# Shifting the SBUF start addresses of the dense products' operands in a hybrid RWKV-7 / Conformer backbone

## The chip, the cores and the metric

The kernel runs on one core of a Trainium2 chip. The metric is the device time of one execution in microseconds (us). The kernel before was run three times: 1453.27, 1447.48 and 1452.06 us, median 1452.06. One more execution was taken with the hardware profiler; it is the one that all traces of the kernel before show.

Engines are named as the profile names them: PE is TensorE's matrix product, PEld its weight load, DVE is VectorE, ACT is ScalarE, POOL is GpSimd, SP is SyncE.

## The reference

Two layers over 512 latent tokens of width 1024, with 256 context tokens. Layer 0 (even) is a bidirectional RWKV-7 scan beside a gated short convolution; layer 1 (odd) is a Conformer convolution module. Cut to what matters here:

```python
# layer 0
r, k, v, za, bg, cg, xb, zb = jnp.split(h @ w_in, EVEN_SPLITS, axis=-1)     # 1024 -> 8 * 1024
ya, _, _ = rwkv_seq(rwkv_prep(h, r, k, v, *rw), S_f, S_b, r_k, lnx_w, lnx_b, True)
yb = bg * dwconv(cg * xb, sc_w, seg_len)
y = jnp.concatenate([ya * jax.nn.silu(za), yb * jax.nn.silu(zb)], axis=-1) @ w_out   # 2048 -> 1024
...
# layer 1
u, gl, z = jnp.split(h @ w_in, 3, axis=-1)                                  # 1024 -> 3 * 2048
a = u * jax.nn.sigmoid(gl)
a = dwconv(a, dw_w, seg_len) + dw_b                                         # 31 taps, segments of 64
a = layer_norm(a, ln_w, ln_b)
return (jax.nn.silu(a) * jax.nn.silu(z)) @ w_out                            # 2048 -> 1024
```

Each layer is wrapped in RMS norms with shift, scale and gate, and the context tokens take part in layer 0 as the scan's prefix.

## The kernel before

**Split-value products.** Most dense products are made from operands that are split into a high part, rounded to the type fp32r, and a low part, the rest (`hilo`, L121). `mm3` (L59) makes one product from three matmuls: high x high, high x low, low x high, all into one PSUM bank. `mm(o, lhsT, rhs)` (L56) issues one matmul: `lhsT` is the stationary operand, which a weight load brings into the array, and `rhs` is the moving operand, which is streamed past it. The trace writes a matmul as output <- moving, stationary. A dense product moves 512 columns past a 128x128 weight (256 columns for the context). While one matmul streams, the next one's weights are loaded.

**Stages, in the order of the program.**
- Start: norms, modulation, and the low-rank projections of layer 0.
- Layer 0's projections (`proj`, L361). The weights are loaded, split (`load_w`, L356) and stationary; the split input `hlat` (`hlh`, `hll`, L201) moves. Outputs are named `plr`, `plk`, `plv`, `pza`, `pcg`, `pxb`, `pbg`, `pzb`, and `pck`, `pcv` for the context. From about 200 us they are placed between the small matmuls of the scan (`chain_ctx`, `chain_lat`, L738), which run chunk by chunk for eight pairs of heads.
- Layer 0's output projection in two halves (`outproj`, L130, output `o`): the weights `wh`, `wl` move, the activations `y` are stationary.
- Layer 1's input projection of `u` and `gl` (`products`, L1119, output `pu`): four column blocks n times four token blocks m, 48 matmuls each; the weights `wc..` move, `h1h` and `h1l` are stationary.
- The 31-tap convolution as a transform, a product and a transform back (`dft_stages`, L1085), one (n, m) block behind the products: `forward` (output `px`) with stationary `dfc` (its high part `dfh` and its low part `dfl`) and moving `ah`, then `back` (output `pc`). `late` takes one of the two after each half of `products`.
- Transposes (`at`), then layer 1's `z` projection in 16 column blocks (L1186, output `pz`): the weights `wz..` are stationary and `h1h`, `h1l` move. Block 0's weights come from the pool tag `wb`, those of blocks 1 to 15 from the tag `wz`.
- The last projection (L1215, output `f`): the weights `wf..` move, the 16 activations `y` are stationary; the first ten of these lie in the tag `wb`, the others in `xr`.

**Forward transform.** `ah` holds 64 tokens of one segment as a high part in one half of its 128 rows and as a low part in the other half; `dfc` holds the same 64 rows of the transform twice. For each of two segments s, one matmul of `dfh` over all 128 rows gives high x (high + low), and one of `dfl` over 64 rows gives low x high. The two 64-row matmuls use different halves of the rows.

**What sets the order.** Within a stage the order of PE is that of the code; some products are held to a written order (`pinned`) or to an anchor (`issue_after`). A weight load or a matmul waits by semaphore for the casts of its operands.

**What sets the addresses.** A tile's start in SBUF, in bytes within each partition, follows from the pools: each pool takes tiles one after another, the pools `cp`, `cvp`, `wk` and `lp` from the left end, `hlp`, `wp`, `op` and `lq` from the right end. One float more or less in a tile shifts all that come after it. These are the places of the dense products' operands in the program before, as the start of the operand modulo 128 bytes:

| output | matmuls | moving | stationary |
|---|---|---|---|
| projections of the latent tokens | 1536, 512 columns | 96 | 96 |
| projections of the context | 384, 256 columns | 96 | 96 |
| `lwl`, `lal` (low-rank weights) | 64 | 96 | 64 |
| `o` | 372 (and 12 others) | 96 | 96 (64 and 32) |
| `pu` | 768 | 32 | 64 |
| `px` high | 32 | 64 | 64 |
| `px` low | 32, of 64 rows | 64 | 28 |
| `pz` block 0 | 24 | 64 | 32 |
| `pz` blocks 1 to 15 | 360 | 64 | 64 |
| `f`, first ten activations | 240 | 64 | 32 |
| `f`, last six | 144 | 64 | 96 |

The small fp32 matmuls of the scan read most operands at 64 or 0, and some, the tiles `E` among them, at 32 or 96.

Of the kernel before, what the change touches and what calls it, by code (L numbers as in the profile page):

```python
# [8 lines left out]
F32 = mybir.dt.float32  # L9
F32R = mybir.dt.float32r  # L10
# [5 lines left out]
P = 128  # L16
# [12 lines left out]
NPROD = 119  # L29
# [22 lines left out]
def kernel(ctx: ExitStack, tc: tile.TileContext, I: dict, out: bass.AP):  # L52
    nc = tc.nc
    V, S, G, T = nc.vector, nc.scalar, nc.gpsimd, nc.tensor
# [4 lines left out]
    def mm3(o, ah, al, bh, bl, start, stop, go=mm):  # L59
        go(o, ah, bh, start, False)  # L60
        go(o, ah, bl, False, False)
        go(o, al, bh, False, stop)
# [4 lines left out]
    def const(name, shape, dt=F32):  # L67
        return cp.tile(shape, dt, tag=name, name=name)

    ident = const("ident", [P, P])  # L70
    epsr = const("epsr", [P, 3])
    G.memset(epsr[:, 0:1], RMS_EPS)
    G.memset(epsr[:, 1:2], LN_EPS)
    G.memset(epsr[:, 2:3], GN_EPS)
    nc.sync.dma_start(ident, I["ident"])

    colsrc = {
# [40 lines left out]
    def bank(name, tag):  # L118
        return ps.tile([P, 512], F32, tag=tag, name=name, bufs=2 if tag in ("at", "zo") else 1)

    def hilo(src, raw, hi, lo, eng=nc.sync):  # L121
        if eng:
            eng.dma_start(raw if len(src.shape) == 2 else raw.rearrange("p (k c) -> p k c", c=src.shape[2]), src)
        else:
            raw = src
        S.copy(hi, raw)  # L126
        env["lo"].tensor_tensor(out=lo, in0=raw, in1=hi, op=ALU.subtract)  # L127
        return hi, lo

    def outproj(m0, tags, ks, held, early=lambda k: (None, None, None), between={}):  # L130
        acc = [[bank(f"o{m0 + m}{n}", tags[2 * m + n]) for n in range(2)] for m in range(2)]
        for k in ks:
            y, yr, ws = early(k)
            if y is None:
                y = op.tile([P, 512], F32R, tag="y", name=f"y{m0}_{k}", bufs=4)
            yh, yl = y[:, 0:256], y[:, 256:512]
            if (m0, k) == (0, 7):
                hilo(oT7[:, 0:256], None, yh, yl, None)
            else:
                if yr is None:  # L140
                    yr = op.tile([P, 256], F32, tag="yr", name=f"yr{m0}_{k}", bufs=4)
                hilo(ysp[k, :, m0 * P : m0 * P + 2 * P], yr, yh, yl)
            if k not in held:
                if ws is None:
                    ws = [op.tile([P, D], F32, tag="wr", name=f"wr{m0}_{k}", bufs=3)] + [
                        op.tile([P, D], F32R, tag="w", name=f"w{x}{m0}_{k}", bufs=6) for x in "hl"]
                held[k] = hilo(wo[k * P : (k + 1) * P, :], *ws)
            wh, wl = held[k]
            for m in range(2):
                ms = slice(m * P, (m + 1) * P)  # L150
                for n in range(2):
                    ns = slice(n * 512, n * 512 + 512)
                    mm3(acc[m][n], yh[:, ms], yl[:, ms], wh[:, ns], wl[:, ns], k == ks[0], k == ks[-1])
            if k in between:
                between[k]()
        return acc
# [10 lines left out]
    def ps_at(name):  # L167
# [3 lines left out]
    hlp = rs.enter_context(tc.tile_pool(name="hlp", bufs=1, reuse_waits="tile", side="right"))  # L171
# [2 lines left out]
    NBUF = {"tmp": 3, "bon": 3, "AR": 6, "BK": 2, "BKt": 4, "UV": 2, "E": 2, "PC0": 4, "PC1": 4, "rnq": 2,  # L174
            "H": 2}
    SIZE = {"AR": D, "BK": 1536, "BKt": D, "UV": 2 * D, "O": 768, "X": D, "E": 4 * D, "P": 528, "H": 256, "HP": 256,
            "h0": 256, "PC0": 8, "PC1": 8, "rnq": 48, "xtmp": 136}

    def w(tag, name, dt=F32):
        return wk.tile([P, SIZE.get(tag, 512)], dt, tag=tag, name=name, bufs=NBUF.get(tag, 1))  # L180
# [4 lines left out]
    def small(name, shape):  # L185
        return cvp.tile(shape, F32, tag=name, name=name)

    ones = small("ones", [P, 1])
    G.memset(ones, 1.0)
    omu, hmu, hka, oka = (small(n, [P, k]) for n, k in (("omu", 24), ("hmu", 24), ("hka", 8), ("oka", 8)))  # L190
    owa, hwa = (small(n, [P, 16]) for n in ("owa", "hwa"))
    blk = small("blk", [P, P])
# [6 lines left out]
    ss6 = small("ss6", [P, 16])  # L199
    lorl = [[cvp.tile([P, SEQ], F32R, tag=f"{t}{z}", name=f"{t}{z}") for z in range(2)] for t in ("tanhl", "xal")]  # L200
    hlat = tuple(hlp.tile([P, KT, SEQ], F32R, tag=t, name=t) for t in ("hlh", "hll"))  # L201
    E0 = w("E", "hctx", F32R).rearrange("p (a k c) -> p a k c", a=2, k=KT)
    hch, hcl = E0[:, 0], E0[:, 1]
    E1 = w("E", "ectx")
# [356 lines left out]
    def pinned():  # L561
        prev = []

        def go(o, lhsT, rhs, start=True, stop=True, op=mm):
            e = op(o, lhsT, rhs, start, stop)
            if prev:
                tc.add_manual_dep(e.ins, prev[-1].name,
                                  mybir.DependencyInfo(mybir.DependencyClass.NoSync, mybir.DependencyReason.DATA),
                                  reason="written order")
            prev[:] = [e.ins]  # L570
            return e

        return go
# [344 lines left out]
    for s in range(12):  # L918
# [10 lines left out]
        for x in STAGE[s >= 4]:  # L929
# [17 lines left out]
            elif x == "C":  # L947
                conv_branch(s - 3, st["anchor"])
                if s == 10:
                    rs.close()  # L950
                    op = rs.enter_context(tc.tile_pool(name="op", bufs=1, reuse_waits="tile", side="right"))
# [20 lines left out]
    def early(k):  # L972
        i = ORDER.index(k)
        tag = etags[i] if i < len(etags) else None
        if tag is None:
            return None, None, None
        y = yr = None
        if i < 4:
            y = w(("kk", "kd", "a", "P")[i], f"ye{k}", F32R)[:, 0:512]
            yr = w(("lwl", "k_", "r_", "lwl")[i], f"yre{k}")[:, 0:256]  # L980
        if tag == "E":
            if not eE:
                e = w("E", "wE", F32R)
                eE.extend([e[:, (2 * j + x) * D : (2 * j + x + 1) * D] for x in range(2)] for j in range(2))
            hl = eE.pop(0)
        else:
            hl = [w(tag, f"we{k}{x}", F32R) for x in "hl"]
        return y, yr, [w("BK", f"wre{k}")[:, 0:D]] + hl

    acc0 = outproj(0, ("mm0", "mm1", "at", "at"), ORDER, held, early)  # L990
    l0.close()
    with ExitStack() as l1:
        lp = l1.enter_context(tc.tile_pool(name="lp", bufs=1, reuse_waits="tile"))
# [2 lines left out]
        def lt(tag, name, dt=F32):  # L996
            return (lq if tag in ("xr", "pr") else lp).tile([P, 512 if tag in ("a", "pr") else D], dt, tag=tag, name=name,
                                                            bufs=BUFS[tag])
# [5 lines left out]
        def big(name, shape, dt=F32):  # L1004
            return lp.tile(shape, dt, tag=name, name=name)
# [10 lines left out]
        def gate_rows(layer):  # L1016
            g = lq.tile([P, D], F32, tag="gg", name="gg1") if layer else lt("wz", "gg0")
            nc.gpsimd.dma_start(g, gvd[layer].unsqueeze(0).to_broadcast([P, D]))
            return g
# [42 lines left out]
        gg = gate_rows(0)  # L1062
        ordered = []
        dfw = lt("a", "dfw")[:, :NPROD]
        dfc = big("dfc", [P, 2 * NPROD + 2], F32R)
        dfh, dfl = dfc[:, :NPROD], dfc[:, NPROD : 2 * NPROD]
        dbe = big("dbe", [P, 8])[:NPROD, 0:1]
        dinv = big("dinv", [NPROD, 64])
        nc.gpsimd.dma_start(dfw, I["dfw"])
        S.copy(dfh, dfw)  # L1070
# [10 lines left out]
        tp = pinned()  # L1081
# [3 lines left out]
        def dft_stages(n, m, ahl):  # L1085
            pr = [lt("pr", f"pr{n}{m}{s}") for s in range(2)]

            def forward():
                px = [bank(f"px{n}{m}{s}", "zo") for s in range(2)]
                for s in range(2):  # L1090
                    tp(px[s][:NPROD], dfh, ahl[s], True, False)
                for s in range(2):
                    tp(px[s][:NPROD], dfl[64 * s : 64 * s + 64, :], ahl[s][64 * s : 64 * s + 64, :], False, True)
                for s in range(2):
                    V.scalar_tensor_tensor(out=pr[s][:NPROD], in0=px[s][:NPROD], scalar=dbe[:, 0:1],  # L1095
                                           in1=What[:, n * 512 : n * 512 + 512], op0=ALU.add, op1=ALU.mult)

            def back():
                pc = bank(f"pc{n}{m}", "at")
                for b in range(2):  # L1100
                    bs = slice(256 * b, 256 * b + 256)
                    for s in range(2):
                        tp(pc[64 * s : 64 * s + 64, bs], dinv, pr[s][:NPROD, bs])
                cr = cres[m][n // 2][:, (n % 2) * 512 : (n % 2) * 512 + 512]
                S.copy(cr, pc)
                V.bn_stats(stats[:, m, n, :], cr)

            return forward, back
# [44 lines left out]
        lq = rs.enter_context(tc.tile_pool(name="lq", bufs=1, reuse_waits="tile", side="right"))  # L1153
# [47 lines left out]
            ys.append((yh, yl))  # L1201
        w2 = I["od_w_out"][0]
        gg = gate_rows(1)
        xres = [lt("wa", f"xo{m}") for m in range(4)]
        for m in range(4):
            nc.gpsimd.dma_start(xres[m], x1d[m])
# [119 lines left out]
```

## Time and profile before

| | |
|---|---|
| three runs, median | 1452.06 us (1447.48 to 1453.27) |
| profiled execution, its own time | 1451.59 us |
| profiled execution, span from first to last instruction | 1449.6 us |
| mean granted TensorE clock | 0.979 |

The span is the time between the first and the last instruction; the execution's own time is 2.0 us longer. Stages by the first start of their matmuls: `pck` at 48.7 us, `pcg` from 489.6 us, `o` from 929.0 us, `pu` from 1040.2 us, `pz` from 1255.5 us, `f` from 1353.4 us. The last store ends the span at 1449.6 us.

Durations of single matmuls in the trace overlap, since the next one starts before the last column of the one before has left the array, and their ends are modelled. How fast a stream of matmuls runs is therefore read from start to start, or from the length of a run of them on the chain divided by their count.

### The profile page before, as it was taken

The page shows a single profiled execution, that of the slowest core. Times are in us where ns is not written, and L with a number is a line of the kernel's source. Part 1 is how long each engine was busy: PE and PEld are TensorE (multiplying, and loading weights), DVE is VectorE, ACT ScalarE, POOL GpSimd, SP SyncE. Part 2 cuts the span into 40 slices and gives each one's busy share as a digit, 9 for nine tenths or more (in the row PEclk, how much of TensorE's full clock was granted, in tenths as well). Part 3 has the DMA queues.
Part 4 walks back from the last instruction along what each step waited for, and adds up shares of the span by engine and source line. Part 5 has one row for each costly group of instructions (what it writes and reads, how often), then busy time and mean ns, then how long its engine had stood idle before and what let it go on. Part 6 is the DMA issues. An engine that isn't in the chain of part 4 may idle for free. (4 is left out here: it accounts for less than half of the span.)

```text
span 1449.6 us, 29729 instructions
## 1 busy us (share of the span) xinstructions
PE 1407.2 (97%) x11921; PEld 1012.7 (70%) x11921; DVE 983.7 (68%) x2294; ACT 749.5 (52%) x1516; POOL 118.2 (8%) x246
## 2 busy tenths in 40 slices
PE   6999999999998999999999999999999999999998
PEld 1564677878776766666676666778777777788876
DVE  2675597568688989999999998557745544544333
ACT  4536364364664665756666565456753323464222
POOL 2023210000101101011011100010000000000000
PEclk9999999979897999999999999999999999999999
DMA  9755433312222321222222212359803303133322
GB/s 324 221 172 160 153 110 98 97 52 71 83 85 74 92 69 59 81 86 60 76 67 83 91 49 84 131 175 324 252 34 102 117 22 95 58 102 91 99 89 86
DMA packets 137626, 158.54 MB, mean 109 GB/s; under 512 B 15375, under 2 KB 104143, under 8 KB 137369
## 3 DMA queue, kind: packets, MB, share of 16 engines
q1 hardware_dynamic: 121104, 106.47, 23.6%
q0 software_dynamic: 15312, 48.99, 10.5%
q8 instruction: 94, 1.54, 0.4%
q10 hardware_dynamic: 1072, 1.19, 0.2%
q14 instruction: 44, 0.36, 0.1%
HBM read 138.33 MB, written 18.28 MB: 108 GB/s over the span
## 5 line engine op out<-in xcount | busy, mean ns | idle before, releaser
L57 PE MATMUL o<-wh,y 128*128 128x512 f32 x248 | 79.7, 397 | 0.0
L658 DVE TENSOR_TENSOR Yl<-Yl,xtmpl 128x126 f32<-128x126 f32 (+22 forms) x248 | 62.2, 251 | 2.7
L656 DVE TENSOR_TENSOR xtmpl<-Xl,Yl 128x126 f32<-128x126 f32 (+22 forms) x248 | 62.0, 250 | 2.7
L57 PE MATMUL pal<-ARl,BKl 64*128 64x128 f32 x512 | 57.8, 306 | 5.5 <-DVE xtmpc L656 2.8
L57 PEld LDWEIGHTS pal<-ARl,BKl 64*128 64x128 f32 x512 | 42.9, 195 | 24.9 <-issue 6.0
L1140 ACT CAST ah<-a 64x512 fp32r<-64x512 f32 x32 | 19.8, 619 | 75.6 <-DVE a L1135 75.2
L57 PE MATMUL zol<-UV,E 64*64 64x64 f32 (+1 forms) x1024 | 54.0, 221 | 0.2 <-ACT UV L764 0.2
L57 PEld LDWEIGHTS o<-wh,y 128*128 128x128 f32 x248 | 45.9, 188 | 9.5
L764 ACT COPY UV<-uh 64x128 f32<-64x128 f32 x128 | 33.3, 260 | 33.5 <-PE uh L57 25.9
L57 PE MATMUL o<-wl,y 128*128 128x512 f32 x124 | 49.4, 398 | 1.2 <-DVE wl L127 1.2
L57 PE MATMUL zol<-Hl,ARl 64*64 64x64 f32 x896 | 50.2, 230 | 0.3
L57 PEld LDWEIGHTS zol<-Hl,ARl 64*64 64x64 f32 x896 | 35.0, 133 | 20.3 <-issue 16.7
L127 DVE TENSOR_TENSOR wl<-wr,wh 128x1024 fp32r<-128x1024 f32 x28 | 34.2, 1223 | 19.6 <-ACT wh L126 19.1
L1135 DVE TENSOR_TENSOR a<-pu,a 128x512 f32<-128x512 f32 x16 | 11.0, 690 | 53.0 <-PE pu L57 50.7
L57 PEld LDWEIGHTS uh<-UV,BKt 128*64 128x64 f32 x704 | 26.7, 138 | 28.5 <-ACT UV L764 23.1
L601 DVE TENSOR_TENSOR E<-pal,maskE 128x512 f32<-128x512 f32 x64 | 43.0, 685 | 3.4 <-PE pal L57 3.0
L57 PEld LDWEIGHTS zol<-UV,E 64*64 64x64 f32 (+1 forms) x1024 | 42.3, 136 | 2.5 <-ACT UV L764 2.0
L1095 DVE SCALAR_TENSOR_TENSOR pr<-px,dbe,What 119x512 f32<-119x512 f32 x32 | 22.6, 745 | 31.1 <-PE px L57 31.1
L126 ACT CAST wh<-wr 128x1024 fp32r<-128x1024 f32 x28 | 29.6, 1056 | 20.7 <-PE o L57 10.4
L771 DVE SCALAR_TENSOR_TENSOR Hl<-uh,PCl,HPl 128x64 f32<-128x64 f32 x112 | 26.4, 277 | 20.1 <-PE uh L57 9.6
L875 POOL DMA_DIRECT2D mwr<-in_mod_w_dram x56 | 29.9, 538 | 114.2 <-PE uh L57 67.4
L57 PE MATMUL uh<-UV,BKt 128*64 128x64 f32 x704 | 36.7, 234 | 2.2 <-ACT UV L764 2.2
(947 smaller groups left out, 4250.9 us busy)
## 6 DMA issues: line engine op xcount, KB each, us to landing
mwr<-in_mod_w_dram POOLq DMA_DIRECT2D x56, 256.0 KB, 3.6
wr<-in_ev_w_out_dram SPq DMA_DIRECT2D x28, 512.0 KB, 5.6
ectx<-in_mod_w_dram SPq DMA_DIRECT2D x12, 512.0 KB, 5.2
wrk<-in_ev_w_in_dram SPq DMA_DIRECT2D x16, 256.0 KB, 3.1
wrv<-in_ev_w_in_dram SPq DMA_DIRECT2D x16, 256.0 KB, 4.6
wrr<-in_ev_w_in_dram SPq DMA_DIRECT2D x16, 256.0 KB, 2.9
wrza<-in_ev_w_in_dram SPq DMA_DIRECT2D x16, 256.0 KB, 2.8
wrcg<-in_ev_w_in_dram SPq DMA_DIRECT2D x16, 256.0 KB, 2.8
```

What stands on the lines that cost most here:

```text
L57: return T.matmul(o, lhsT, rhs, start=start, stop=stop)
L126: S.copy(hi, raw)
L127: env["lo"].tensor_tensor(out=lo, in0=raw, in1=hi, op=ALU.subtract)
L601: V.tensor_tensor(out=E[:, h, z * NLAT + c0 : z * NLAT + c0 + m, :], in0=pas[h], in1=maskE[:, z * (1 + h) : z * (1 + h) + 1, 0:x].to_broad ...
L656: V.tensor_tensor(out=tv, in0=X[:, :i, i : i + 1].to_broadcast([P, i, m]), in1=Y[:, i : i + 1, c0:].to_broadcast([P, i, m]), op=ALU.mult)
L658: V.tensor_tensor(out=Y[:, :i, c0:], in0=Y[:, :i, c0:], in1=tv, op=ALU.add)
L764: u_ = S.copy(UV[ZR[1 - h], i : 2 * nch - i : 2 * nch - 1 - 2 * i, ZR[h]], uh[ZR[1 - h], 0:2, :])
L771: h_ = V.scalar_tensor_tensor(out=Hn[:, z, :], in0=uh[:, 2 + z, :], scalar=PC[z][:, i : i + 1], in1=HP[:, z, :], op0=ALU.mult, op1=ALU.add)
L875: nc.gpsimd.dma_start(mws[q], I["mod_w"][layer, kt * P : (kt + 1) * P, c0 : c0 + 512])
L1095: V.scalar_tensor_tensor(out=pr[s][:NPROD], in0=px[s][:NPROD], scalar=dbe[:, 0:1], in1=What[:, n * 512 : n * 512 + 512], op0=ALU.add, op1= ...
L1135: V.tensor_tensor(out=a, in0=pp[1], in1=a, op=ALU.mult)
L1140: S.copy(ahl[s][hr], a[hr])
```

## The change

Three kinds of edits. First, tiles are added, moved or given another width so that what comes after them in their pools starts elsewhere: `epsr` gets a fourth column, which takes the place of the tile `ones`; `xtmp` grows from 136 to 144 floats; `dfc` from 240 to 256, `dbe` from 8 to 32; and each of the right-hand pools `hlp`, `op` and `lq` gets a tile of 8 floats that nothing reads or writes. Second, `ones` is set by POOL as that fourth column, ahead of the other constants' load. Third, the two low products of the forward transform use all 128 rows of `dfl` and of `ah`, so that they give low x (high + low).

```diff
-    epsr = const("epsr", [P, 3])
+    epsr = const("epsr", [P, 4])
...
+    ones = epsr[:, 3:4]
+    G.memset(ones, 1.0)
...
-            "h0": 256, "PC0": 8, "PC1": 8, "rnq": 48, "xtmp": 136}
+            "h0": 256, "PC0": 8, "PC1": 8, "rnq": 48, "xtmp": 144}
...
-    ones = small("ones", [P, 1])
-    G.memset(ones, 1.0)
...
     hlat = tuple(hlp.tile([P, KT, SEQ], F32R, tag=t, name=t) for t in ("hlh", "hll"))
+    hlp.tile([P, 8], F32, tag="pad", name="padh")
...
     acc0 = outproj(0, ("mm0", "mm1", "at", "at"), ORDER, held, early)
+    op.tile([P, 8], F32, tag="pad", name="pado")
...
-        dfc = big("dfc", [P, 2 * NPROD + 2], F32R)
+        dfc = big("dfc", [P, 256], F32R)
         dfh, dfl = dfc[:, :NPROD], dfc[:, NPROD : 2 * NPROD]
-        dbe = big("dbe", [P, 8])[:NPROD, 0:1]
+        dbe = big("dbe", [NPROD, 32])[:, 0:1]
...
                 for s in range(2):
-                    tp(px[s][:NPROD], dfl[64 * s : 64 * s + 64, :], ahl[s][64 * s : 64 * s + 64, :], False, True)
+                    tp(px[s][:NPROD], dfl, ahl[s], False, True)
...
         gg = gate_rows(1)
+        lq.tile([P, 8], F32, tag="pad", name="padq")
```

The number of instructions on each engine, their order and the semaphores that they wait for are the same in both programs. In the program after, the operands of all products in the table above start at 64 modulo 128, moving and stationary alike, with two exceptions: the stationary `dfl` still starts at 28, and the 12 other `o` products have 64 and 0. The operands of the scan's small matmuls then start at 0 or 64 as well, so at 0 modulo 64.

## The prediction

> **What bounds the kernel now.** I read the page first, then the stages, then the chain of work that ended last, then single matmuls in order of time.
>
> ```profile
> span 1449.6 us, 29729 instructions
> PE 1407.2 (97%) x11921; PEld 1012.7 (70%) x11921; DVE 983.7 (68%) x2294; ACT 749.5 (52%) x1516; POOL 118.2 (8%) x246
> 500.00:900.00 400.00, 391.88 (x5185) 270.43 (x5183) 366.36 (x1046) 252.03 (x595) 40.73 (x73) 1.00 0.25 75
> 1050.00:1250.00 200.00, 200.00 (x897) 146.83 (x896) 97.93 (x127) 75.29 (x114) 1.05 (x2) 1.00 0.22 70
> 1354.00:1443.00 89.00, 89.00 (x381) 71.12 (x380) 27.88 (x36) 23.04 (x35) 0.00 (x0) 1.00 0.25 80
> ```
>
> The last three rows are windows: span, then busy time of PE, PEld, DVE, ACT, POOL, then the granted clock, the DMA share and GB/s. From 500 to 900 us, where the scan's chains run, PE and DVE are both nearly full, and which of them sets the pace cannot be read from busy time. From 1050 us on it can: PE is busy all the time at the full clock, and the other engines and the DMA are half idle or less. The chain says the same:
>
> ```profile
> 968.54 31.52 PE o L57 x138
> ...
> 1073.46 5.80 PE pu L57 x24
> 1079.25 1.01 PE pc L57 x8
> 1080.27 5.80 PE pu L57 x24
> 1086.06 0.89 PE px L57 x4
> 1086.95 5.79 PE pu L57 x24
> ...
> 1284.61 68.94 PE pz L57 x304
> 1353.56 90.10 PE f L57 x384
> ```
>
> Columns are start, length, engine, output and count. From 1040 us to 1444 us hardly anything but matmuls stands on the chain, one after another. **In this third of the span a nanosecond off one matmul is a nanosecond off the time.** Now divide length by count. `f`: 90.10 / 384 = 234.6 ns each. `pz`: 68.94 / 304 = 226.8 ns. Both move 512 columns through a 128x128 weight at the full clock, so one of them loses 8 ns per matmul. `o`, 31.52 / 138 = 228.4 ns with the start of its run included, is near the fast kind.
>
> **Where the 8 ns are.** By the table of start addresses above, `pz` from the second output block on has both operands at 64 modulo 128; `o` has both at 96; `pu` has 32 against 64; `f` has 64 against 32 or 96. So the fast kinds have moving and stationary operand at the same place modulo 64, and the slow kinds lie 32 bytes apart. Single matmuls in order of time (start, length, engine, line, operation; output <- moving, stationary):
>
> ```profile
> 83.14 0.39 PE L57 MATMUL plv<-hll,whv 128*128 128x512 f32 x1
> ...
> 85.41 0.39 PE L57 MATMUL plv<-hlh,wlv 128*128 128x512 f32 x1
> ...
> 1075.82 0.39 PE L57 MATMUL pu<-wc002l,h1h 128*128 128x512 f32 x1
> ...
> 1077.45 0.40 PE L57 MATMUL pu<-wc004h,h1l 128*128 128x512 f32 x1
> ...
> 1257.18 0.39 PE L57 MATMUL pz<-h1h,wz0h 128*128 128x512 f32 x1
> 1257.41 0.40 PE L57 MATMUL pz<-h1l,wz0h 128*128 128x512 f32 x1
> 1257.65 0.40 PE L57 MATMUL pz<-h1h,wz0l 128*128 128x512 f32 x1
> 1257.89 0.39 PE L57 MATMUL pz<-h1h,wz0h 128*128 128x512 f32 x1
> ...
> 1339.79 0.39 PE L57 MATMUL pz<-h1h,wz13h 128*128 128x512 f32 x1
> ...
> 1341.83 0.39 PE L57 MATMUL pz<-h1h,wz13h 128*128 128x512 f32 x1
> ```
>
> Starts are divided by steps. `plv` (96 and 96): 10 steps in 2.27 us, 227 ns. `pu` (32 and 64): 7 steps in 1.63 us, 233 ns. `pz13` (64 and 64): 9 steps in 2.04 us, 226.7 ns. The best control is `pz0`: the same loop, the same shapes, the same moving tile as `pz13`, but its weights come from another pool tag and lie at 32. It takes 0.71 us for 3 steps, 237 ns (these follow another product at once). Role does not matter (`o` and `pu` both move weights past activations, and only `pu` is slow), nor does 96 against 64 (`plv`, `pz13`). What is left is the distance modulo 64 between what PE streams and what its weight load reads meanwhile.
>
> A rule speaks against this reading. The Trainium skill, page "TensorE: Matmul & The Clock Gate", section "Step-by-step: what each phase is for", says: "Loading the next tile's weights doesn't steal SBUF read bandwidth from the running matmul." By it, operand addresses would not matter, the first three terms below would be nothing, and the first rival would hold. The trace does not agree, with 237 against 226.7 ns inside one loop.
>
> **The change, part by part.** The order of the instructions and their waits is the same on every engine, so nothing passes anything; only addresses and one pair of shapes differ. DVE and ACT do the same operations on moved tiles, and the DMAs the same packets.
>
> 1. `pu`: 768 products go from 233 to 226.7 ns. 6.2 ns x 768 = 4.8 us, all on the chain.
> 2. `f`: 384 products go from 234.6 to 226.7 ns. 7.9 ns x 384 = 3.0 us, all on the chain.
> 3. `pz0`: 24 products, some 6 ns each, 0.1 us. The 64 products of the low-rank weights (`lwl`, `lal`) would give 0.4 us more, but they lie in the stages with a full DVE; I count nothing.
> 4. The 1,908 products at 96 and 96 (projections, `o`) move to 64 and 64. Both already step at 227 ns: nothing. The 384 half-width ones likewise.
> 5. The forward transform. Its four matmuls are two of 128 rows and two of 64 rows, the latter on different halves of the array:
>
> ```profile
> 1072.42 1.04 PE L57 MATMUL px<-ah,dfc 128*119 128x512 f32 x4
> 1073.39 0.50 PE L57 MATMUL pu<-wc000h,h1h 128*128 128x512 f32 x1
> 1073.73 0.39 PE L57 MATMUL pu<-wc000l,h1h 128*128 128x512 f32 x1
> ...
> 1072.96 0.18 PEld L57 LDWEIGHTS px<-ah,dfc 64*119 64x119 f32 x2 [0.36 <-issue]
> 1073.38 0.19 PEld L57 LDWEIGHTS pu<-wc000h,h1h 128*128 128x128 f32 x1 [0.24 <-issue]
> ```
>
> The lower two rows are weight loads. The load of the half-row pair does not start while a full-row product runs (0.36 us idle before it), nor does the load of the full-row product after the pair (0.24 us). From the first `px` to the second `pu` it takes 1073.73 - 1072.42 = 1.31 us for five matmuls. Five full-row ones in a stream take 3 x 226.7 + 2 x 233 = 1.15 us; I give the two low ones the slow step, since their stationary still starts at 28 modulo 64. That saves 0.16 us, 16 times: 2.6 us. Bounds: at best 5 x 226.7 = 1.13 us, 2.8 us in all. At worst neither of the two pauses goes, and only the pair is replaced: it took 1073.38 - 1072.96 = 0.42 us, two full-row ones take 0.47, so 0.05 x 16 = 0.8 us are lost. I take 2.6, since the pauses stand only where the height of the rows changes.
>
> 6. The memset of `ones` moves to another tile, and `dbe` and `xtmp` grow by a few bytes: nothing, since POOL works 1.05 us in 200. If a later start of the first gates were to follow, it would be under a microsecond.
>
> Sum: 4.8 + 3.0 + 0.1 + 2.6 = **10.5 us**. The profiled execution took 1451.6 us (span 1449.6), 0.5 us under the median of the three runs, 1452.06. 1451.6 - 10.5 = 1441.1; I say 1441, or 0.8% less. No cover is used up: at 1050 to 1250 us the DMA share is 0.22, and at 1354 to 1443 us 0.25, so weights still arrive ahead of a PE that is 3% faster there.
>
> **Rivals.**
>
> *Address has no part in it.* Then `pu` and `f` are slow for a reason that I do not see, and only the transform gains: 1451.6 - 2.6 = 1449. Against it stands `pz0` beside `pz13`. For it: `pz0` is eight k-tiles just after a transform, and there is only one such control.
>
> *The transform loses.* The pauses stay, and its term is +0.8 instead of -2.6: 1451.6 - 7.9 + 0.8 = 1444.5. For it: `px` also waits for its operand at times, which looks the same. Against: the loads stand idle exactly ahead of the change of rows.
>
> *The middle gains too.* In the chain stages a dense product follows small ones some 300 times, and the steps after a switch need a while to settle:
>
> ```profile
> 621.85 0.40 PE L57 MATMUL pxb<-hll,whxb 128*128 128x512 f32 x1
> 622.08 0.39 PE L57 MATMUL pxb<-hlh,wlxb 128*128 128x512 f32 x1
> 622.31 0.40 PE L57 MATMUL pxb<-hlh,whxb 128*128 128x512 f32 x1
> 622.54 0.39 PE L57 MATMUL pxb<-hll,whxb 128*128 128x512 f32 x1
> 622.77 0.39 PE L57 MATMUL pxb<-hlh,wlxb 128*128 128x512 f32 x1
> 623.00 0.39 PE L57 MATMUL pbg<-hlh,whbg 128*128 128x512 f32 x1
> ```
>
> Five steps take 1.15 us against 5 x 226.7 = 1.13, so some 20 ns a switch, 6 us in all. Most small operands lie at 64, the dense ones at 96, and the change brings them together. If that were the reason, and PE set the pace there, the time would be 1435. Against it: DVE is 92% busy there (366.36 of 400 us), and products in unbroken runs at 96 are as fast as at 64.
>
> *The clock (slower).* Three stretches of the context stage run at a reduced clock:
>
> ```profile
> 300.00:330.00 30.00, 27.08 (x335) 23.28 (x334) 17.58 (x31) 14.98 (x31) 1.08 (x2) 0.72 0.12 38
> 380.00:402.00 22.00, 20.58 (x261) 16.65 (x261) 13.68 (x20) 11.54 (x21) 1.67 (x3) 0.69 0.26 73
> 446.00:470.00 24.00, 22.93 (x273) 17.04 (x275) 17.66 (x36) 10.00 (x22) 1.63 (x3) 0.57 0.23 75
> ```
>
> The clock lost is 0.28 x 30 = 8.4 us, 0.31 x 22 = 6.8 us and 0.43 x 24 = 10.3 us of PE time at most. Slightly different gaps there may add or remove such a stretch. One more leaves 1441 + 8.5 = 1449.5; it decides from two more on, 1441 + 17 = 1458, slower than before. Against it: the stage's order is unchanged, its products already have the fast step, and the three runs lie within 5.8 us (1447.48 to 1453.27).
>
> **How the numbers follow.** Forecast 0.70, address without effect 0.08, transform loses 0.06, middle gains 0.12, clock 0.04. The likeliest time is 1441. The range goes from 1435 (the middle's price) to 1448 (a clock stretch or most of the first rival's loss). A measurement of this kernel can tell about 0.5%, or 7.3 us, from no change, so the border is 1444.8. Faster by more: nearly all of the forecast (0.65, since its margin is 3.7 us), the middle's 0.12, and half of the transform's 0.06, 0.80 together. Slower by more: 0.03. Within: 0.17.
>
> **What the profile after would show.** Chain: `pu` x24 at 5.55 us in place of 5.80, `f` x384 at 87.1 in place of 90.1, `pz` x304 still 68.9, `px` x4 still about 0.9 but with the step from the last `px` to the first and second `pu` at 0.23 each in place of 0.34. Timeline: `pu` steps of 227 ns. The 64-row weight loads and their idle time are gone. Windows: the stage from 1040 to 1254 us shorter by 7.4 us, the `f` stage by 3.0, and 500 to 900 us unchanged. The prediction is wrong if `pu` still steps at 233 ns with both operands at 64, if `px` costs more than 1.31 us with the `pu` after it, or if the time up to 1040 us moves by more than 3 us.

## The result, and the profile after

| | before | after |
|---|---|---|
| timed runs | 9 | 9 |
| median | 1450.53 us | 1441.82 us |
| lowest to highest | 1447.48 to 1453.27 us | 1436.65 to 1449.40 us |
| ratio of after to before, 95% interval | | 0.9945 [0.9921, 0.9969] |
| profiled execution, its own time | 1451.59 us | 1449.03 us |
| its mean granted clock | 0.979 | 0.974 |

The forecast was 1441.0 us, from 1435 to 1448. The median lies 0.8 us above it. The profiled execution of the changed kernel is only 2.6 us under that of before, though, and ran at a lower clock; that has to be read first.

The page after, whole span:

```profile
span 1447.1 us, 29729 instructions
PE 1404.1 (97%) x11921; PEld 1020.5 (71%) x11921; DVE 983.7 (68%) x2294; ACT 749.1 (52%) x1516; POOL 118.0 (8%) x246
```

The instructions are as many as before, and DVE is busy to the tenth of a microsecond as long as before. Windows of the program after (columns as in the prediction):

```profile
300.00:330.00 30.00, 27.08 (x335) 23.23 (x334) 17.60 (x31) 15.01 (x32) 1.08 (x2) 0.72 0.14 39
446.00:480.00 34.00, 32.98 (x365) 24.11 (x367) 21.58 (x50) 15.41 (x34) 1.62 (x3) 0.55 0.19 63
575.00:583.00 8.00, 7.37 (x45) 4.88 (x45) 6.89 (x27) 3.56 (x7) 0.00 (x0) 0.79 0.22 66
500.00:900.00 400.00, 392.01 (x5130) 271.25 (x5129) 365.97 (x1039) 251.49 (x590) 42.44 (x76) 1.00 0.25 75
```

And two of the same windows in the program before:

```profile
575.00:583.00 8.00, 7.77 (x112) 5.93 (x111) 7.90 (x26) 7.13 (x13) 0.00 (x0) 1.00 0.32 91
446.00:480.00 34.00, 32.94 (x427) 24.25 (x428) 25.22 (x62) 17.74 (x39) 2.16 (x4) 0.70 0.22 69
```

The seventh number is the granted clock. From 446 to 480 us it is 0.55 after against 0.70 before, and from 575 to 583 us 0.79 against 1.00. In the record of the clock, the stretch at half clock that begins at 447.9 us is 30.7 us long after and 20.5 us before, and one of 3.4 us at 577.6 us is new; the three earlier ones are the same in both (6.8, 17.1 and 13.7 us). So this one execution had 13.6 us more at half clock. The stages, by the first start of their matmuls, show where the time went:

| stage | before | after | difference |
|---|---|---|---|
| start to first `pu` | 1040.2 us | 1046.1 us | +5.9 (the clock) |
| first `pu` to first `pz` | 215.3 | 209.5 | -5.8 |
| first `pz` to first `f` | 97.9 | 97.7 | -0.2 |
| first `f` to the end of the last | 90.2 | 87.8 | -2.4 |
| rest | 6.0 | 6.0 | 0 |

The last third, where PE sets the pace, is 8.5 us shorter (by the unrounded times); the forecast had 10.5. The chain of work that ended last, in the changed kernel:

```profile
1072.12 5.71 PE pu L57 x24
1077.83 0.92 PE px L57 x4
1078.75 5.46 PE pu L57 x24
1084.21 1.01 PE pc L57 x8
1085.23 5.71 PE pu L57 x24
...
1284.47 68.93 PE pz L57 x304
1353.40 80.21 PE f L57 x351
```

`pz` is as before (68.94 us there). `f` takes 80.21 / 351 = 228.5 ns, against 234.6 before. `pu` has two lengths now: 5.46 us, that is 24 x 227.5 ns, after a forward transform, and 5.71 us after a transform back. Before, both were 5.80.

### The profile page after: what moved, and what is told of

Its sections match the earlier page's. It is cut to its first block, busy times and chain, and to the rows that moved or that the text cites. A ratio compares the mean times of both kernels' runs of the same rounds, so it can differ in the third digit from the quotient of the medians.

```text
span 1447.1 us, 29729 instructions
## 1 busy us (share of the span) xinstructions
PE 1404.1 (97%) x11921; PEld 1020.5 (71%) x11921; DVE 983.7 (68%) x2294; ACT 749.1 (52%) x1516; POOL 118.0 (8%) x246
```

## The experiments

The times below come from several groups of runs, each with runs of the kernel before on the same chip. "Step" is the mean from one 512-column matmul's start to the next one's, of those that waited for nothing. "Start to `pz`" is the time from the first `pu` to the first `pz`, which the clock did not touch in any of these profiles.

**e1_rows**: the program before, with the full-row low products alone.

```diff
-                    tp(px[s][:NPROD], dfl[64 * s : 64 * s + 64, :], ahl[s][64 * s : 64 * s + 64, :], False, True)
+                    tp(px[s][:NPROD], dfl, ahl[s], False, True)
```

> The kernel before with one edit: the two low products of the forward transform use all 128 rows; all addresses as before. Theory (the loads pause where the height of the rows changes): first px to second pu takes 1.15 us in place of 1.31, the stretch from the first pu to the first pz shrinks by 16 x 0.16 = 2.5 us from 215.3 to 212.8, pu still steps at 233 ns, f and pz unchanged, time 2.5 us under the kernel before (ratio 0.998). Rival (the pauses are px waiting for its operand): first px to second pu stays at 1.31 us or grows by 0.05, time 0 to 0.8 us above. Until 1040 us the run is that of the kernel before, granted clock 0.979 included.

Median of 12 runs 1449.16 us, ratio 0.9986 [0.9964, 1.0009]. Start to `pz`: 213.1 us (215.3 before). Chain of e1_rows:

```profile
1064.64 5.79 PE pu L57 x24
1070.43 0.92 PE px L57 x4
1071.36 5.61 PE pu L57 x24
...
1349.22 90.10 PE f L57 x384
```

Only the `pu` run behind `px` became shorter, 5.61 in place of 5.79 us: the pause before its first two matmuls is gone. `px` itself costs 0.04 us more (0.92 for 0.88). `f` did not move. So the pauses do go, and this part alone brings 2.2 us of the stage. The rival by which the transform loses falls.

**e2_pads**: the program after, with the low products on 64 rows again, that is, the addresses alone.

```diff
-                    tp(px[s][:NPROD], dfl, ahl[s], False, True)
+                    tp(px[s][:NPROD], dfl[64 * s : 64 * s + 64, :], ahl[s][64 * s : 64 * s + 64, :], False, True)
```

> The changed kernel with the low products of the forward transform back on 64 rows each: the address shift alone. Theory (distance modulo 64 bytes between moving and stationary operand): pu steps of 227 ns in unbroken runs, first pu to first pz 211.9 us (215.3 before, 209.4 changed), f from 1353.4 to its last start shorter by 2.3 us as in the changed kernel, px with its pauses at 1.31 us; time 6 us under the kernel before at the same granted clock (ratio 0.996). Rival (addresses have no part, the transform alone gains): no difference from the kernel before. Second question: if the longer stretches of half clock that the changed kernel's trace shows from 448 us on come with the shifted addresses, they are here too; if they are chance, the granted clock of the runs spreads here as it does in the kernel before.

Median of 12 runs 1442.58 us, ratio 0.9945 [0.9923, 0.9967]. Start to `pz`: 211.9 us. Chain of e2_pads:

```profile
1059.08 5.71 PE pu L57 x24
1064.79 0.88 PE px L57 x4
1065.66 5.67 PE pu L57 x24
...
1342.77 87.68 PE f L57 x384
```

About two thirds of the gain come from addresses: 3.4 us of the stage and 2.4 us of `f`, of 8.5 us in all. The parts nearly add up: -2.2 and -3.4 us give -5.6 for the stage, and both together had -5.8.

**e3_apart32**: the program after with eight floats behind `h1l`. They move what `big` and the pool `lp` hold after them by 32 bytes: the weights of `u`, `gl` and `z`, of `f` too, and ten of the `y`, while `h1h`, `h1l` and the tiles of `lq` stay.

```diff
         h1l = big("h1l", [P, KT, SEQ], F32R)
+        big("padx", [P, 8])
```

> The changed kernel with a tile of 8 floats between h1l and all later tiles of the pool lp: in pu the moving operand lies at 96 and the stationary at 64, in pz (all 16 blocks) the moving at 64 and the stationary at 96, in the last six activations of f 96 and 64, in the first ten of f both at 96. Theory: pu back to 233 ns, pz up from 226.8 to 233 ns, f slow only in its last six activations; time 768 x 5 + 384 x 6.5 + 144 x 7 = 3.8 + 2.5 + 1.0 = 7.3 us above the changed kernel at the same clock. Rival (something else than the distance made pu and f slow, and the shift removed it): pz stays at 226.8 ns and pu at 227 to 228, the time is that of the changed kernel.

Median of 10 runs 1448.76 us, ratio 0.9987 [0.9961, 1.0013]. Chain of e3_apart32:

```profile
1060.04 5.79 PE pu L57 x24
...
1066.76 5.60 PE pu L57 x24
...
1275.68 70.94 PE pz L57 x304
1346.62 88.39 PE f L57 x384
```

One unused tile takes the gain of the addresses away and leaves that of the transform: 5.79 and 5.60 are e1's lengths. `pz`, fast in both programs, lost 2.0 us (70.94 / 304 = 233.4 ns). In `f`, the ten activations that moved with the weights step at 227.1 ns, and the six that stayed at 233.2. The rival by which the address has no part falls.

**e4_apart64**: the same with 16 floats, so that the operands lie 64 bytes apart. By the prediction's rule, distance modulo 64, nothing would be lost.

```diff
+        big("padx", [P, 16])
```

> As e3_apart32 with 16 floats: the operands of pu, of pz and of the last six activations of f lie 64 bytes apart modulo 128 (0 against 64), those of the first ten of f both at 0. Theory A (the distance counts modulo 64): all steps stay at 227 ns, the time is that of the changed kernel. Theory B (it counts modulo 128, so that 64 is a distance too): pu, pz and part of f slow as in e3_apart32, 7.3 us above the changed kernel.

Median of 10 runs 1444.18 us, ratio 0.9959 [0.9935, 0.9984]. Chain of e4_apart64:

```profile
1062.14 5.72 PE pu L57 x24
...
1068.80 5.50 PE pu L57 x24
...
1275.55 70.93 PE pz L57 x304
```

Neither theory gave this. `pu` steps at 229.2 ns, nearly free, and `pz` at 233.3 ns, with the full loss, both at 64 bytes. The rule modulo 64 is wrong. Three things differ between the two: the role (in `pu` the weights that moved are streamed, in `pz` they are stationary), the sign of the distance, and the place of each operand.

**e6_flip**: the place. The tiles of `lp` from `h1h` on lie 64 bytes further than in e4: `h1h` and `h1l` start at 0 modulo 512 and the weights at 64, where e4 had 448 and 0. Role and sign stay.

```diff
+        big("pady", [P, 16])
         h1h = big("h1h", [P, KT, SEQ], F32R)
         h1l = big("h1l", [P, KT, SEQ], F32R)
+        big("padx", [P, 16])
```

> The changed kernel with h1h and h1l at 0 modulo 128 and all else of the pool lp at 64: in pu the moving operand at 64 and the stationary at 0, in pz the moving at 0 and the stationary at 64. With 64 bytes between them the other way round (e4_apart64) pu stepped at 229.5 ns and pz at 233.3. Theory A (which of the two lies at 0 decides: moving at 64 with stationary at 0 is slow, the reverse nearly free): pu 233, pz 229 to 230, time 768 x 5 + 384 x 2 = 4.6 us above the changed kernel at the same clock. Theory B (the kind of loop decides, addresses 64 bytes apart being equal): pu 229.5 and pz 233.3 again, 3.3 us above. f stays at 227.

Median of 10 runs 1444.79 us, ratio 0.9949 [0.9927, 0.9972]. Chain of e6_flip:

```profile
1062.49 5.72 PE pu L57 x24
...
1275.92 70.94 PE pz L57 x304
1346.87 88.31 PE f L57 x384
```

`pu` (229.2 ns) and `pz` (233.3) did as in e4 though each operand's own place had changed. So what falls is every theory by which the place of one operand decides. The last six activations of `f` were expected to stay at 227 ns and went to 232.6: they now lie 128 bytes from the weights. That missed number pointed to a period longer than 64 or 128 bytes.

**e8_apart256** and **e9_apart128**: 64 and 32 floats, so 256 and 128 bytes. In both, the operands start at 64 modulo 128 as in the changed kernel, and by that rule both would be fast.

```diff
+        big("padx", [P, 64])
...
+        big("padx", [P, 32])
```

> The changed kernel with a tile of 64 floats after h1l: every start in the table is still 64 modulo 128, but in pu the moving operand lies 256 bytes past the stationary modulo 512, in pz 256 before it, in the last six activations of f 256 past, in the first ten of f at the same place. Steps sorted by the distance modulo 256 over all runs so far: 0 gives 227 ns, 64 gives 229, and 32, 96, 160, 192 and 224 give 233 to 234. Theory (modulo 256): all steps stay at 227. Rival (modulo 512, as all fast pairs so far agree modulo 512 too): pu, pz and the last six activations of f leave 227 for 229 to 234 ns.

> As e8_apart256 with 32 floats, a distance of 128 bytes: the starts are still 64 modulo 128 everywhere. The rule that the front table was read by (equal modulo 64, or modulo 128) says that all steps stay at 227 ns. Theory (modulo 256): pu, pz and the last six activations of f go to some 233 ns, as the last six of f did at this distance in e6_flip (232.6), pz x304 from 68.9 to 70.9 us, and the first ten of f stay at 227.

One execution each: 1437.21 and 1445.28 us, beside 1444.34 for the kernel before (clocks 0.985, 0.984, 0.983). Chain of e8_apart256:

```profile
1060.28 5.71 PE pu L57 x24
...
1066.91 5.46 PE pu L57 x24
...
1272.62 68.95 PE pz L57 x304
1341.57 87.69 PE f L57 x384
```

Chain of e9_apart128:

```profile
1242.47 5.58 PE pu L57 x24
...
1278.03 70.92 PE pz L57 x304
1348.96 88.38 PE f L57 x384
```

At 256 bytes everything is fast; at 128 `pz` has the full loss and `pu` steps at 232.7 ns.

**e10_apart192**: role or sign. With 48 floats the weights lie at the other side of `h1h` and `h1l`, 64 bytes off modulo 256 as in e4.

```diff
+        big("padx", [P, 48])
```

> The changed kernel with 48 floats behind h1l. The weights of u, gl and z, those of f and the first ten y then lie 192 bytes (that is -64 modulo 256) from h1h and h1l, in place of +64 as with 16 floats. Sign of the distance (moving minus the stationary loaded meanwhile, modulo 256): pu has 192 and steps at 233 ns (24 behind px 5.58 to 5.60 us), pz has 64 and steps at 229 ns (304 in 69.6 us), the last six of f have 192 and step at 233. Role (a moving weight may lie 64 away, a stationary weight may not): pu and the last six of f at 229 ns as with 16 floats (24 behind px 5.50 us), pz at 233 (304 in 70.9 us). Both: the first ten of f at 227 ns, distance 0.

One execution: 1446.09 us, beside 1455.19 for the kernel before (clocks 0.982 and 0.976). Chain of e10_apart192:

```profile
1064.44 5.79 PE pu L57 x24
...
1071.17 5.60 PE pu L57 x24
...
1280.07 69.60 PE pz L57 x304
1349.67 88.40 PE f L57 x384
```

The two have changed sides: `pu` loses (233.2 ns), `pz` is nearly free (228.9), with the lengths that the expectation gave for the sign. The role has no part.

All steps now, by the distance modulo 256 bytes of the moving operand from the stationary operand that is loaded meanwhile (moving minus stationary):

| distance | seen in | mean step |
|---|---|---|
| 0 | `pu`, `pz`, `f`, `o` of after and e8 | 226.8 to 228.5 ns (the upper end is `pu`, with its settling steps, below) |
| 32 | `pu` and part of `f` in e3 | 233.2 to 233.4 |
| 64 | `pu` and part of `f` in e4, `pu` in e6, `pz` in e10 | 228.9 to 229.2 |
| 96 | `pu` before | 233.1 |
| 128 | part of `f` in e6; `pu`, `pz` and part of `f` in e9 | 232.6 to 233.2 |
| 160 | `f` before, first ten | 234.3 |
| 192 | `pz` in e4 and e6; `pu` and part of `f` in e10 | 233.2 to 233.3 |
| 224 | `pz` in e3; `f` before, last six | 233.2 |

These are all the multiples of 32. All tiles of these programs start at multiples of 32 bytes, so a float more moves what follows only when the tile needs 32 bytes more: `epsr` grew from 12 to 16 bytes and moved nothing, while dropping the tile `ones` did. Of finer distances only 36 was seen, in two `px` steps (e5, below).

The table of starts modulo 128 in the section on the kernel before hides one thing. Modulo 256 the context's projections have 96 (moving) and 224 (stationary) before, and 64 and 192 after: 128 bytes apart in both programs. Their steps of 256 columns take 120 ns in both (median of `pcv`). Half of 227 would be 113.5, an estimate from the 512-column steps. So these 384 products seem to lose some 6 ns each as well, and the change left that; no run here puts them at distance 0 or shows what else may bound so short a step.

**e5_dfl**: the one operand that the change left at 28 is moved to the place of the others.

```diff
-        dfh, dfl = dfc[:, :NPROD], dfc[:, NPROD : 2 * NPROD]
+        dfh, dfl = dfc[:, :NPROD], dfc[:, 128 : 128 + NPROD]
```

> The changed kernel with the low part of the transform's matrix at a distance of 128 floats from the high part, so that dfl starts at 64 modulo 128 too (28 before). In the changed kernel's trace the four px of a block step at 226, 234, 235 and 227 ns: the second, whose own stationary is dfh at 64, is slow, and the fourth, whose own stationary is dfl at 28, is fast. Theory (what counts is the weight load that runs beside a stream, so that of the next matmul): second and third fall to 227 ns, the first and fourth stay. Rival (the own stationary counts, or the start of a transform is slow anyway): second stays at 234. Either way 16 x 0.015 = 0.2 us, which the time cannot show; the time is that of the changed kernel, 9 us under the kernel before at equal granted clock.

Median of 6 runs 1441.70 us, ratio 0.9922 [0.9893, 0.9952]. Start to `pz`: 208.9 us, 0.6 less than after. Chain of e5_dfl:

```profile
1068.62 0.91 PE px L57 x4
1069.52 5.44 PE pu L57 x24
```

In the changed kernel the second and third of a block's four `px` steps took 234 and 235 ns and the first and fourth 226 and 227; here they take 227, 227, 226 and 227. The fourth was fast although its *own* stationary lies at 28, and the second slow although its own lies at 64. What counts is the weight that is loaded *while* a matmul streams, the next one's. That is how the table above was made. The two slow steps stream `ah` at 64 modulo 128 while `dfl` at 28 is loaded, a distance of 36.

**e7_pairs**: e5, with the transforms back of two blocks put next to each other (`pr` has four buffers, and every second place in `late` takes two of them), because 5.71 against 5.46 us says that each change to `pc` and back costs the next `pu` run 0.25 us.

```diff
+        backs = []
+        def queue(f, b):
+            backs.append(b)
+            late.append(f)
+            late.append((lambda two: lambda: [x() for x in two])(backs[-2:] if len(backs) % 2 == 0 else []))
```

> e5_dfl with the transforms back of two blocks put next to each other, after every second block (four pr tiles in place of two). Each transform back costs a pause where pu gives way to it (318 to 326 ns in place of 227) and where pu follows (340), and some ten settling steps that are 60 ns over 227 each in all. Theory (a pause belongs to each change of the tile's shape on PE): 8 changes each way are saved, 8 x (0.10 + 0.11 + 0.06) = 2.2 us in the stretch from the first pu to the first pz, and the second transform back follows the first without a pause; time 2 us under e5_dfl. Rival (each transform back pays for its own start, whatever comes before it): no gain, and the later end of the second one delays the transposes.

Median of 8 runs 1440.89 us, ratio 0.9926 [0.9895, 0.9957]. Chain of e7_pairs:

```profile
1076.51 5.44 PE pu L57 x24
1081.95 1.88 PE pc L57 x16
1083.83 5.66 PE pu L57 x24
...
1090.40 10.88 PE pu L57 x48
```

Sixteen `pc` take 1.88 us, less than twice 1.01, and a `pu` run of 48 with no `pc` in it steps at 226.7 ns. From the first `pu` to the end of the last `pz`, 305.3 us against 306.7 in e5: 1.5 us less, where 2.2 were expected. (To the first `pz`, the stretch that the expectation named, it is 205.7 against 208.9 us, but 16 `pc` stand behind the first `pz` here and 8 in e5, so part of that is work put off.) Part of the gain went to new waits: the chain has four pieces of DMA that e5 has not, for `wc200`, `wc206`, `wc300` and `wc306`, and three `px` steps grew to 412, 499 and 469 ns. Against the changed kernel itself the medians differ by 0.9 us, which is within their scatter; at equal clock (next table) it is 2.1 ± 1.6 us.

**The clock, from all timed runs.** Each run lists its mean granted clock, from 0.974 to 0.987 for the kernel before and from 0.974 to 0.985 for the changed one. A least-squares fit over 131 timed runs (54 of the kernel before, the rest of eight other kernels), with one level for each kernel and one slope for all, gives 1.09 us for each 0.001 of the clock, and leaves 1.7 us of scatter. (The single executions of e8, e9 and e10 are not in it.) Differences from the kernel before at equal clock, with 95% intervals:

| kernel | difference, us |
|---|---|
| after | -9.2 ± 1.2 |
| e1 (transform alone) | -2.6 ± 1.0 |
| e2 (addresses alone) | -6.7 ± 1.0 |
| e3 (32 apart) | -2.3 ± 1.1 |
| e4 (64 apart) | -4.8 ± 1.1 |
| e6 (64 apart, both moved) | -5.2 ± 1.1 |
| e5 (`dfl` moved too) | -9.0 ± 1.4 |
| e7 (and transforms back in pairs) | -11.3 ± 1.2 |

The groups ran on different chips; the medians of the kernel before in the three groups of several runs are 1450.53, 1450.53 and 1451.57 us. Nothing here sets the clock, so this is a comparison and not an experiment. It agrees with the stages: -8.5 us in the profiled pair. The means of the clock are alike (0.980 to 0.982), and the kernel before has runs at 0.974 too (1461.89 and 1460.79 us among them). So nothing ties the long stretch at half clock in the profile of after to the change.

## Why the prediction was right, and where its steps were off

**The bound** was right. From 1040 us on PE sets the pace, and what a step loses or gains stands in the time. From 500 to 900 us the busy times stayed: PE 391.88 and 392.01 us, DVE 366.36 and 365.97. That window is at fixed times, so it can't show a shorter stage. But at equal clock the whole gained 9.2 ± 1.2 us and the stages from `pu` on 8.5, which leaves 0.7 ± 1.2 for all that comes earlier. The rival by which the middle gains 6 us more falls.

**The control.** The prediction leaned most on `pz0` beside `pz13`, 237 against 226.7 ns. It was weaker than it looked. In the changed kernel, with both operands at the same place, the same three steps still take 230 ns, and the five free `pz0` steps ahead of them, behind a transform back, 235 (233 before). Over all its free steps `pz0` went from 232.7 to 230.9 ns. So a part of its slowness was not of address but the settling described under term 1. That the reading held all the same was partly luck: what shows it are e3 to e10, where the other 15 blocks change too.

**Term 1, `pu`, 4.8 us: measured about 3.4.** The stage gained 5.8 us, of which the transform had 2.4 (below). Steps do fall from 233 to 227 ns, but not all. The timeline after, behind a transform back (starts, lengths):

```profile
1084.14 1.08 PE L57 MATMUL pc<-pr,dinv 119*64 119x256 f32 x8
1085.16 0.50 PE L57 MATMUL pu<-wc010h,h1h 128*128 128x512 f32 x1
1085.50 0.40 PE L57 MATMUL pu<-wc010l,h1h 128*128 128x512 f32 x1
1085.74 0.40 PE L57 MATMUL pu<-wc010h,h1l 128*128 128x512 f32 x1
1085.97 0.40 PE L57 MATMUL pu<-wc010h,h1h 128*128 128x512 f32 x1
...
1087.60 0.39 PE L57 MATMUL pu<-wc012l,h1h 128*128 128x512 f32 x1
1087.83 0.39 PE L57 MATMUL pu<-wc012h,h1l 128*128 128x512 f32 x1
```

The first step takes 340 ns, and then ten take 1087.83 - 1085.50 = 2.33 us, 233 ns each, with all operands at the same place. Only after that comes 227. These eleven steps, some 15 times, at 6 ns are 1.0 us, and five behind each `px` another 0.4: what the term is short of. The prediction quoted this settling, in the chain stages, and used it for a rival only; it belonged in this term. In e5, with `dfl` in place, the settling after `px` is gone (24 steps in 5.44 us); after `pc` it stays (5.71). Why it takes some ten steps is open.

**Term 2, `f`, 3.0 us: measured 2.4.** The step of 226.9 ns came out as forecast. But 234.6 was the run's length over its count, and held three waits; without them the step before was 233.9. So 7.0 ns x 383 = 2.7 us. The waits, 0.28 us in all before, grew to 0.55. The casts start when earlier products of `f` are done (ACT's cast of `wf140h` waited 4.4 us for PE) and take as long as before, 1.05 us on ACT and 1.23 us on DVE, while PE now needs less time for the products between. Timeline of the changed kernel:

```profile
1387.92 0.39 PE L57 MATMUL f<-wf120h,y 128*128 128x512 f32 x1
1388.22 0.50 PE L57 MATMUL f<-wf140l,y 128*128 128x512 f32 x1
```

One tile there, `wf140l`, in the view of what is done with it:

```profile
L129 DVE TENSOR_TENSOR wf140l<-wf140r,wf140h x1: 1226/1226/1226, 1386.9 to 1386.9; 128x1024 fp32r<-128x1024 f32 x1
```

The low part is ready at 1386.9 + 1.23 = 1388.1 us, and the weight load waits for it. "No cover is used up" was said of DMA; it should have been asked of the casts too.

**Term 3, `pz0`**, 0.1 us: 0.2 from first `pz` to first `f`, a stretch that holds the end of the transforms too; 24 steps at 1.8 ns less are 0.04 of it. **Term 4**, 96 and 96 to 64 and 64: nothing, as forecast. For the half-width products the reason was off, though: they lie 128 bytes apart modulo 256 before and after, and by the estimate above they were not fast already. **Term 5**, the transform, 2.6 us: 2.6 ± 1.0 in e1 at equal clock, and by the stages 2.2 (e1 against before) and 2.4 (after against e2). The pauses did stand at the change of the rows' height. **Term 6**, the moved memset: the start does not differ; the first `pck` starts at 48.7 us in both programs, and the first `lwl` at 426.7 us in both.

**The rule.** "Distance modulo 64" was right for every pair that the prediction compared and wrong as a rule. None of these lay 64 or 128 apart; all were 0 or an odd multiple of 32, so they could not show the period. (The context's projections, 128 apart, were there to be seen, but the table gave their places modulo 128.) e4 and e9 break it; e8 and e9 together give modulo 256. In the program after, nearly all dense operands of 512-column products start at 448 modulo 512 (not those of `lwl`, `lal` and 12 of `o`), so the change works by more than the 64 modulo 128 that its description names; e9 keeps that and is slower than the changed kernel by 3.1 us up to `pz`, 2.1 in `pz` and 0.7 in `f`. The sentence that was weighed there from the Trainium skill, page "TensorE: Matmul & The Clock Gate", section "Step-by-step: what each phase is for", that loading the next weights doesn't take SBUF read bandwidth from the running matmul, doesn't hold in these runs: with the load at another place modulo 256, and nothing else changed, `pz` steps at 233.2 ns in place of 227.1 (e9, e8). What the two have to share at such distances, no run shows.

**The clock**, a rival at 0.04: the mechanism is real, and the profiled execution met it (+5.9 us up to `pu`). By that the prediction's own sign of being wrong, more than 3 us there, was met in this one execution. The stretch is not brought by the change, so far as 131 runs tell, and it moves both kernels.

The errors of the terms (1.4 us too much for `pu`, 0.6 for `f`, 0.2 for the transform, 0.1 to 0.2 too little for the stretch of `pz0`) make some 8.5 us of 10.5 in the profiled pair; at equal clock over all runs it is -9.2 ± 1.2. The forecast of 1441.0 lies that near to 1441.82 also because the median of before came out 1.1 us under the profiled execution that the sum started from.

## What to carry to other kernels

Where PE is busy without a gap, divide the length of a run of matmuls by its count and compare the loops: 227 against 233 ns, with the same shapes, was 0.5% of this kernel, and a few unused floats brought it. Put the moving operand and the stationary operand that is loaded while it streams at the same start modulo 256 bytes, and check the distance again after every change of a tile's size. Keep small tile shapes together, since a change of shape slows some ten steps behind it and not only the first.

## What the hardware showed that was not expected

- The loss depends on the distance modulo 256 bytes, and at 64 bytes on its sign: 64 costs 2 ns of a step, 192 (that is -64) costs 6.3 (e4, e10).
- It depends on the *next* stationary operand, not on the matmul's own (e5).
- After a transform back of 119 x 64 tiles, the first full step takes 340 ns and some ten more 233 ns, with operands in the good place, before 227 is reached.
- Stretches at half clock come in multiples of 3.4 us (3.4, 6.8, 10.2, 13.7, 17.1, 20.5 and 30.7 us seen), at about the same places of the program and in other lengths from run to run; 0.001 of the mean clock is worth 1.09 us here. What sets their length was not tried.
